# Turning each query and key tile once: high and low parts side by side, and copies that write both halves of the partitions

## The chip, the cores and the metric

The kernel runs on one core of a Trainium2 chip. The core has TensorE (PE, matrix products; PEld is its weight load), VectorE (DVE), ScalarE (ACT), GpSimd (POOL) and SyncE (SP, which issues most DMAs). SBUF is the working memory of 128 partitions, PSUM the memory of 8 banks into which PE writes. The metric is the device time in microseconds of one execution, the median of several runs.

## The reference

A two-layer backbone block on 512 latent tokens and 256 context tokens, model width 1024, head width 64. Layer 0 has two groups of heads, windowed with a sink (A) and dense (B), each with grouped queries (four query heads for one key and value head); layer 1 is differential attention with eight heads of two sub-heads. Queries and keys are normalised by their root mean square and rotated before the scores:

```
# layer 0, per group of four query heads (A; B is dense and has no sink)
qa = _rms(qa.reshape(b, n, HEADS_A, d), qn_a);  ka = _rms(ka.reshape(b, n, KV_A, d), kn_a)
qa, ka = _rope(qa, cos, sin), _rope(ka, cos, sin)
s = einsum('bqhgd,bkhd->bhgqk', q, k) * scale;  o = softmax(s) @ v
# layer 1, two sub-heads a = 0, 1 per head
s = einsum('bqhad,bkhad->bhaqk', q, k) * scale
p = softmax(s);  o = (p[:, :, 0] - lam * p[:, :, 1]) @ v
```

Each layer ends in a SwiGLU feed-forward network; all inputs and outputs are fp32.

## The kernel before, in words

All products that need more than the reduced precision of one pass are split: an operand x is held as a high part (rounded to the type fp32r) and a low part, x minus the high part. For the scores the split is folded into the contraction. A head has only 64 dimensions, so the 128 partitions of a turned tile hold two copies or two parts of the same 64 numbers. In layer 0 the query tile qt holds [high; low] along the partitions, and the key tile kT holds for j = 0 the high part of the key twice, [high; high], and for j = 1 the low part twice, [low; low]; two products with the same qt and j = 0, 1 (line 578) add up all four combinations. In layer 1 it is the other way round: kT holds [high; low] for each sub-head, and qt holds [high; high] and [low; low] (lines 715 and 716).

The tiles are made as follows. A projection (project, line 465) writes 128 tokens x 384 columns into a PSUM bank; ACT copies it to SBUF (qkv, lines 520 and 677); DVE and POOL normalise and rotate it (qy). ACT rounds the high part into qd or kd, and DVE (queries) or POOL (keys) subtracts it to get the low part (lines 525 to 530 and 685 to 689). PE then turns 128 tokens x 128 numbers at a time by a transpose against the identity identr into PSUM (qpt and kpt, lines 535, 543, 696, 702), and ACT copies the turned tile to SBUF (lines 537, 544, 698, 703), where the scores read it as qt and kT.

The order of PE's instructions is written out by hand from layer 0's sixth attention step to the end; the other engines' orders come from a planner that takes the instructions in program order as they become ready. In layer 0 one step of attention (attend0: scores into sc, softmax, four probability tiles turned into ppt and copied to Pt, values) is interleaved with quarters of the next head group's projection; a list `due` holds the turns of queries and keys (turn_q, turn_k), and one is taken at fixed places between the quarters. In layer 1 the loop over 32 steps (8 heads x 4 tiles of queries) takes in turn the scores, half a projection, the transposes of the probabilities of the step before (ppt, line 734), half a projection, its values (av, line 744), a turn (turned, which runs the function transposes of a projected tile), half a projection, and another turn.

PSUM is shared by tags: `tr_tile` hands out the banks tr0 and tr1 in turn, and qpt, kpt and layer 1's ppt take theirs from it; in layer 0 ppt takes tr0 and tr1 by the parity of its chunk (`one=kc % 2`). A bank is given to its next tile only when all readers of the one before are done. The inputs of the scores have room for some steps: six qt tiles in layer 0, five in layer 1.

Of the kernel before, what the change touches and what calls it, by code (L numbers as in the profile page):

```python
# [12 lines left out]
F32R = mybir.dt.float32r  # L13
# [6 lines left out]
P = 128  # L20
# [7 lines left out]
HD = 64  # L28
# [23 lines left out]
def bc(ap, pos, n):  # L52

    dims = [list(d) for d in ap.ap]
    return AP(ap.tensor, ap.offset, dims[:pos] + [[0, n]] + dims[pos:])
# [8 lines left out]
def backbone(es: ExitStack, tc: tile.TileContext, x, c, ctx, c_ctx, mod_w, mod_b, norm_mix_w, norm_ffn_w,  # L64
# [3 lines left out]
    nc = tc.nc  # L68
# [24 lines left out]
    def acc_tile(name, n=512, one=None):  # L93

        if one is None:
            one = turn["acc"] = 1 - turn["acc"]
        return p_1.tile([P, 512], F32, name=name, tag=f"acc{one}")[:, :n]
# [4 lines left out]
    def tr_tile(name, shape, dt=F32, one=None):  # L102
        if one is None:
            one = turn["tr"] = 1 - turn["tr"]
        return p_1.tile(shape, dt, name=name, tag=f"tr{one}")
# [10 lines left out]
    def f32(ap):  # L116
        return ap.bitcast(F32)
# [13 lines left out]
    identr = cp.tile([P, P], F32R, name="identr")  # L131
# [248 lines left out]
    def rope_tables(pool, wq, wk):  # L380

        rp = raw_tile([P, NTX, 2, HD], "rp")
        nc.sync.dma_start(rp, rope)
        w = pool.tile([P, 2, HD], F32, name="rw", tag="rw")
        nc.sync.dma_start(w[:, 0, :], dram_rows(wq))
        nc.sync.dma_start(w[:, 1, :], dram_rows(wk))
        nc.vector.tensor_scalar(w[:, 0, :], w[:, 0, :], HD ** -0.5, None, ALU.mult)
        tb = pool.tile([P, 2, NTX, 2, HD], F32, name="rt", tag="rt")
        for j in range(2):
            nc.vector.tensor_tensor(tb[:, j, :, 0, :], rp[:, :, 0, :], bc(w[:, j, :], 1, NTX), ALU.mult)  # L390
            sw = swap_pairs(w[:, j, :])
            nc.vector.tensor_tensor(tb[:, j, :, 1, :].rearrange("p t (a b) -> p t a b", b=2),
                                    rp[:, :, 1, :].rearrange("p t (a b) -> p t a b", b=2),
                                    bc(sw, 1, NTX), ALU.mult)
        return w, tb
# [64 lines left out]
    def project(ps, t, ws, c0, c1, ks=range(KT), terms=((0, 0), (0, 1), (1, 0))):  # L460

        hs = [tile_T(j, t) for j in range(2)]
        for k in ks:
            for j, z in terms:
                nc.tensor.matmul(ps, hs[j][:, k, :], ws[k // 2][z][:, k % 2, c0:c1], start=(k, j, z) == (0, 0, 0),  # L465
                                 stop=(k, j, z) == (KT - 1, 1, 0))
# [14 lines left out]
    def weights0(b, wp, subs, new_tile=raw_tile, loads=((0, 1), (), (2,), (3,))):  # L481
# [3 lines left out]
        for u in range(4):  # L485
# [13 lines left out]
            subs[u % len(subs)].tensor_sub(lo, raw, f32(hi))  # L499
            yield hi, lo  # L500

    def tables0(j, tabs, wp):
        tabs[j] = rope_tables(wp, *((ev_qn_a[0], ev_kn_a[0]) if j == 0 else (ev_qn_b[0], ev_kn_b[0])))

    def in_proj0(b, ws, tabs, wp, st, later, begun={}):

        kT = st.tile([P, 2, TOK], F32R, name="kT", tag="kT")
        vv = st.tile([P, NT, HD], F32, name="vv", tag="vv")
        qs = {}
        yield qs, kT, vv  # L510
        for t in CTX_FIRST:
            ps = begun[t] if t in begun else acc_tile("inps", 384, one=int(b == 0 and t == CTX_FIRST[-1]))
            for k in range(0, KT, 2):
                if k:
                    yield
                if b == 0 and t in CTX_FIRST[:2]:
                    continue
                project(ps, t, ws, 0, 384, range(k, k + 2))
            raw = wp.tile([P, 384], F32, name="qkv", tag="qkv", bufs=2)
            nc.scalar.copy(raw, ps)  # L520
            nc.gpsimd.tensor_copy(vv[:, t, :], raw[:, 320:384])
            y, r = rotate(raw[:, 0:320], 4, 1, t, *tabs[b // 2], wp)
            nc.gpsimd.tensor_tensor(y, y, bc(r, 2, HD), ALU.mult)
            qd = wp.tile([P, 4, 2, HD], F32R, name="qd", tag="qd", bufs=2)
            nc.scalar.copy(qd[:, :, 0, :], y[:, 0:4])
            nc.vector.tensor_sub(qd[:, :, 1, :], y[:, 0:4], f32(qd[:, :, 0, :]))
            kd = wp.tile([P, 2, 2, HD], F32R, name="kd", tag="kd", bufs=2)
            kb = bc(y[:, 4, :], 1, 2)
            nc.scalar.copy(kd[:, 0], kb)
            nc.gpsimd.tensor_sub(kd[:, 1], kb, f32(kd[:, 0]))  # L530

            def turn_q(t=t, qd=qd):
                pt = tr_tile("qpt", [P, 4, P], F32R)
                for h in range(4):
                    nc.tensor.transpose(pt[:, h, :], qd[:, h].rearrange("p a d -> p (a d)"), identr)
                qt = st.tile([P, 4, P], F32R, name="qt", tag="qt", bufs=6)
                nc.scalar.copy(qt, f32(pt))
                qs[t] = qt

            def turn_k(t=t, kd=kd):  # L540
                pk = tr_tile("kpt", [P, 2, P], F32R)
                for j in range(2):
                    nc.tensor.transpose(pk[:, j, :], kd[:, j].rearrange("p a d -> p (a d)"), identr)
                nc.scalar.copy(kT[:, :, t * P:(t + 1) * P], f32(pk))
            later += [turn_q, turn_k]
            yield

# [109 lines left out]
    class Proj1:  # L657
# [14 lines left out]
        def finish(self, t, ps):  # L672

            n, wp, kT, qs = self.width(t), self.wp.pool, self.kT, self.qs
            m, h0 = (n - P) // HD, 0 if t < NTX else 2
            raw = wp.tile([P, 384], F32, name="qkv", tag="qkv", bufs=4)
            nc.scalar.copy(raw[:, :n], ps[:, :n])  # L677
            nc.gpsimd.tensor_copy(self.vv[:, t, :], raw[:, n - P:n])
            y, r = rotate_all(raw[:, :n - P], h0, m, t, self.wc, self.tb, wp)
            nc.gpsimd.tensor_tensor(y, y, bc(r, 2, HD), ALU.mult)  # L680
            nq = m - 2
            if nq:
                qd = wp.tile([P, 2, 2, 2, HD], F32R, name="qd", tag="qd", bufs=3)
                yb = bc(y[:, 0:2], 2, 2)
                nc.scalar.copy(qd[:, 0], yb)
                nc.vector.tensor_sub(qd[:, 1], yb, f32(qd[:, 0]))
            kd = wp.tile([P, 2, 2, HD], F32R, name="kd", tag="kd", bufs=3)
            nc.scalar.copy(kd[:, :, 0, :], y[:, nq:nq + 2])
            nc.gpsimd.tensor_sub(kd[:, :, 1, :], y[:, nq:nq + 2], f32(kd[:, :, 0, :]))

            def transposes():
                if nq:
                    pt = tr_tile("qpt", [P, 2, 2, P], F32R)
                    for j in range(2):
                        for a in range(2):
                            nc.tensor.transpose(pt[:, j, a, :], qd[:, j, a].rearrange("p a d -> p (a d)"), identr)
                    qt = self.qp.tile([P, 2, 2, P], F32R, name="qt", tag="qt", bufs=5)
                    nc.scalar.copy(qt, f32(pt))
                    qs[t] = qt
                pk = tr_tile("kpt", [P, 2, P], F32R)  # L700
                for a in range(2):
                    nc.tensor.transpose(pk[:, a, :], kd[:, a].rearrange("p a d -> p (a d)"), identr)
                nc.scalar.copy(kT[:, :, t * P:(t + 1) * P], f32(pk))
            return transposes
# [452 lines left out]
    wp = Pool("mw0", "right")  # L1157
# [5 lines left out]
    for t in CTX_FIRST:  # L1163
# [4 lines left out]
        for g in range(2):  # L1168
            pt = tr_tile("npt", [P, 4, P])
# [46 lines left out]
    mods = [(0, part, n) for part in (2, 3, 4) for n in range(4)]  # L1216
    tabs = {}
    tables0(0, tabs, wp.pool)

    start.close()  # L1220
# [6 lines left out]
    even = Pool("even0")  # L1227
    due, made = [], 0
    proj = in_proj0(0, ws, tabs, wp.pool, even.pool, due, begun)
    state = next(proj)  # L1230

# [58 lines left out]
    if True:  # L1290
        for i, (b, t) in enumerate(steps):
            j = i % NT
# [3 lines left out]
            if j == 0 and b < 3:  # L1296
                ws += units
                proj = in_proj0(b + 1, ws, tabs, wp.pool, (even if b % 2 else odd).pool, due)
                nxt = next(proj)
# [30 lines left out]
            if t == 0:  # L1330
# [13 lines left out]
                wp = Pool("w0", "right")  # L1344
# [219 lines left out]
    wp = Pool("mw1", "right")  # L1564
# [44 lines left out]
    if True:  # L1609
# [117 lines left out]
        wp = Pool("w1", "right")  # L1727
# [203 lines left out]
```

## Time and profile before

| what | before |
|---|---|
| median of 3 runs | 1697.77 us (1697.59 to 1698.07) |
| span of the profiled execution, first to last instruction | 1695.6 us |
| what lies around the span, against the median | 2.2 us |
| PE busy | 1631.5 us (96%) |
| DVE busy | 1146.7 us (68%) |
| ACT busy | 937.0 us (55%) |
| POOL busy | 696.4 us (41%) |
| layer 0's attention with its projections | about 60 to 345 us |
| layer 0's feed-forward part and the way out of it | about 345 to 975 us |
| layer 1's attention with its projections | about 975 to 1300 us |

The profile is of one execution; the runs were timed without it, so the profiled execution's own time is taken as its span, and the 2.2 us beside it as constant. Busy time of PE is modelled from pipelined products: a product's duration is its latency, and the distance from one start to the next is what it costs in a full stream.

### The profile page before, as it was taken

To read this page: it belongs to the slowest core of one execution; us is meant where nothing else is said; L and a number is where in the kernel's file an instruction comes from. 1 tells how busy PE (TensorE), PEld (TensorE's weight loads), DVE (VectorE), ACT (ScalarE), POOL (GpSimd) and SP (SyncE) were. 2 spreads that over 40 slices of the span, in tenths; PEclk is the share of its full clock that TensorE was granted. 3 is DMA by queue.
4 is the path that set the end of the run, shared out by engine and by line. 5 is a ranking of instruction groups with operands and counts; after the bars stand their busy time and mean duration, and the time that the engine had idled before them with its cause. 6 is when DMAs were issued, how large, how long until landed. Compare 5 with 4: busy or idle time off the path is not lost. (4 is left out here: it accounts for less than half of the span.)

```text
span 1695.6 us, 28585 instructions
## 1 busy us (share of the span) xinstructions
PE 1631.5 (96%) x10390; PEld 1468.6 (87%) x10390; DVE 1146.7 (68%) x2014; ACT 937.0 (55%) x2011; POOL 696.4 (41%) x867
## 2 busy tenths in 40 slices
PE   6999999899999999999999989999999999999998
PEld 3977787677999999998777889999988899999887
DVE  3765656754799887767767656666666598887434
ACT  5565555745456665545554456666666555555320
POOL 2665554321346554412413366666664242221000
PEclk8999999999999999999999999999999999999999
DMA  9222221411455555439966311111112433331431
GB/s 319 69 71 74 70 70 50 164 60 38 129 167 172 164 159 162 134 108 347 296 184 189 99 43 38 48 42 44 50 45 97 125 93 102 111 101 57 137 99 62
DMA packets 218108, 194.64 MB, mean 115 GB/s; under 512 B 20016, under 2 KB 202864, under 8 KB 217968
## 3 DMA queue, kind: packets, MB, share of 16 engines
q1 hardware_dynamic: 217616, 192.62, 36.8%
q8 instruction: 81, 1.33, 0.3%
q14 instruction: 59, 0.48, 0.1%
q10 hardware_dynamic: 352, 0.21, 0.0%
HBM read 179.92 MB, written 12.87 MB: 114 GB/s over the span
## 5 line engine op out<-in xcount | busy, mean ns | idle before, releaser
L901 ACT CAST wbh<-wr 128x512 fp32r<-128x512 f32 x170 | 104.9, 621 | 130.2 <-PE p L933 73.4
L933 PE MATMUL p<-hT,wbh 128*128 128x256 f32 (+1 forms) x752 | 154.5, 299 | 0.0
L465 PE MATMUL inps<-wih,hT 128*128 128x384 f32 x512 | 144.2, 344 | 7.3 <-ACT qkv L677 7.3
L911 POOL TENSOR_TENSOR wbl<-wr,wbh 128x512 fp32r<-128x512 f32 x43 | 60.0, 1396 | 173.6 <-ACT wbh L901 173.6
L933 PEld LDWEIGHTS p<-hT,wbh 128*128 128x128 f32 x752 | 121.9, 191 | 0.2
L911 DVE TENSOR_TENSOR wbl<-wr,wbh 128x512 fp32r<-128x512 f32 x127 | 107.7, 858 | 21.0 <-ACT wbh L901 16.8
L933 PE MATMUL p<-hT,wbl 128*128 128x256 f32 (+1 forms) x376 | 111.9, 298 | 0.0
L933 PE MATMUL p<-t,wbh 128*128 128x384 f32 (+1 forms) x480 | 111.3, 318 | 0.0
L604 POOL TENSOR_SCALAR Pt<-Pt,rc 128x256 f32<-128x256 f32 (+3 forms) x96 | 74.6, 788 | 89.3 <-DVE rc L601 83.1
L231 POOL TENSOR_TENSOR modp<-modp 128x512 f32<-128x512 f32 x40 | 57.4, 1436 | 114.3 <-ACT modp L230 114.3
L465 PEld LDWEIGHTS inps<-wih,hT 128*128 128x128 f32 x512 | 93.3, 188 | 10.6 <-ACT qkv L677 9.7
L933 PE MATMUL p<-hTt,wbh 128*128 128x256 f32 (+1 forms) x480 | 101.0, 302 | 0.0
L887 POOL TENSOR_TENSOR wr<-wr 128x512 f32<-128x512 f32 x40 | 61.6, 1540 | 89.8 <-DVE ws L892 85.8
L933 PE MATMUL p<-b,wbh 128*128 128x384 f32 x368 | 93.8, 336 | 0.2 <-DVE c L961 0.2
L901 ACT CAST wbh<-ws 128x512 fp32r<-128x512 f32 x120 | 69.4, 579 | 43.1 <-PE p L933 29.0
L224 DVE SCALAR_TENSOR_TENSOR ma<-modw,cols,ma 128x256 f32<-128x256 f32 x140 | 89.2, 637 | 2.3
L592 ACT ACTIVATE Pt<-sc,nm 128x256 f32<-128x256 f32 (+3 forms) x96 | 67.6, 707 | 35.3 <-DVE nm L588 16.9
L465 PE MATMUL inps<-wil,hT 128*128 128x384 f32 x256 | 86.0, 336 | 0.0
L933 PEld LDWEIGHTS p<-t,wbh 128*128 128x128 f32 x480 | 82.9, 189 | 0.0
L911 DVE TENSOR_TENSOR wbl<-ws,wbh 128x512 fp32r<-128x512 f32 x120 | 81.7, 681 | 1.7 <-ACT wbh L901 1.6
L933 PEld LDWEIGHTS p<-hTt,wbh 128*128 128x128 f32 x480 | 78.3, 191 | 3.1 <-ACT modp L230 1.6
L230 ACT ACTIVATE modp<-modw,cols 128x256 f32<-128x256 f32 x160 | 68.4, 500 | 18.0 <-POOL ma L236 10.1
(355 smaller groups left out, 5217.9 us busy)
## 6 DMA issues: line engine op xcount, KB each, us to landing
modw<-in_mod_w_dram SPq DMA_DIRECT2D x96, 512.0 KB, 5.2
wr<-in_ffn_w_in_dram SPq DMA_DIRECT2D x176, 256.0 KB, 2.9
wdr<-in_ffn_w_out_dram SPq DMA_DIRECT2D x66, 512.0 KB, 3.7
wir<-in_od_w_in_dram SPq DMA_DIRECT2D x96, 128.0 KB, 2.3
hidm<-hid SPq DMA_DIRECT2D x44, 192.0 KB, 1.9
hr<-hidm SPq DMA_DIRECT2D x22, 192.0 KB, 3.5
x<-in_x_dram SPq DMA_DIRECT2D x8, 512.0 KB, 3.5
wir<-in_ev_w_in_dram SPq DMA_DIRECT2D x16, 256.0 KB, 3.5
```

The source lines that it names most:

```text
L224: nc.vector.scalar_tensor_tensor(acc, w[:, k], scale[k], acc, ALU.mult, ALU.add)
L230: nc.scalar.activation(pr[:, k], w[:, k], AF.Copy, scale=scale[k])
L231: nc.gpsimd.tensor_add(pr[:, 0:2], pr[:, 0:2], pr[:, 2:4])
L465: nc.tensor.matmul(ps, hs[j][:, k, :], ws[k // 2][z][:, k % 2, c0:c1], start=(k, j, z) == (0, 0, 0), stop=(k, j, z) == (KT - 1, 1, 0))
L592: turn["exp"] = nc.scalar.activation(p[:, :n], s, AF.Exp, bias=nm[:, c1], accum_out=sm[:, c1])
L604: nc.gpsimd.tensor_scalar(p[:, :n], p[:, :n], rc[:, hh:hh + 1], 1.0, ALU.mult, ALU.mult)
L887: nc.gpsimd.tensor_sub(w, raw[f, "G1"], w)
L901: nc.scalar.copy(hi, w)
L911: (nc.gpsimd if name == "G2" else nc.vector).tensor_sub(lo, raw[need[n]], f32(hi))
L933: nc.tensor.matmul(ps, w[:, k, :], H[b][h][:, k, :], start=first and k == 0 and q == 0, stop=final and k == 3 and q == 2, skip_group_check ...
```

## The change

Layer 0's keys and layer 1's queries are no longer doubled before the turn. kd (layer 0) and qd (layer 1) hold the high and the low part side by side, as the other two tiles did before, so that one transpose of 128 numbers turns both parts: [high; low] along the partitions. The doubling is done by the copy out of PSUM. A new function both_halves copies part j (64 partitions of the turned tile) twice: ACT writes it to the half of the partitions in which it lies, DVE to the other half. What the scores read is laid out as before, and PE's order is otherwise the same.

```diff
+    def both_halves(to, pt):
+        for j in range(2):
+            part = f32(pt[HD * j:HD * (j + 1)])
+            nc.scalar.copy(to[HD * j:HD * (j + 1), j], part)
+            nc.vector.tensor_copy(to[HD * (1 - j):HD * (2 - j), j], part)
...
-            kd = wp.tile([P, 2, 2, HD], F32R, name="kd", tag="kd", bufs=2)
-            kb = bc(y[:, 4, :], 1, 2)
-            nc.scalar.copy(kd[:, 0], kb)
-            nc.gpsimd.tensor_sub(kd[:, 1], kb, f32(kd[:, 0]))
+            kd = wp.tile([P, 2, HD], F32R, name="kd", tag="kd", bufs=2)
+            nc.scalar.copy(kd[:, 0], y[:, 4])
+            nc.gpsimd.tensor_sub(kd[:, 1], y[:, 4], f32(kd[:, 0]))
...
             def turn_k(t=t, kd=kd):
-                pk = tr_tile("kpt", [P, 2, P], F32R)
-                for j in range(2):
-                    nc.tensor.transpose(pk[:, j, :], kd[:, j].rearrange("p a d -> p (a d)"), identr)
-                nc.scalar.copy(kT[:, :, t * P:(t + 1) * P], f32(pk))
+                pk = tr_tile("kpt", [P, P], F32R)
+                nc.tensor.transpose(pk, kd.rearrange("p a d -> p (a d)"), identr)
+                both_halves(kT[:, :, t * P:(t + 1) * P], pk)
...
-                qd = wp.tile([P, 2, 2, 2, HD], F32R, name="qd", tag="qd", bufs=3)
-                yb = bc(y[:, 0:2], 2, 2)
-                nc.scalar.copy(qd[:, 0], yb)
-                nc.vector.tensor_sub(qd[:, 1], yb, f32(qd[:, 0]))
+                qd = wp.tile([P, 2, 2, HD], F32R, name="qd", tag="qd", bufs=3)
+                nc.scalar.copy(qd[:, :, 0, :], y[:, 0:2])
+                nc.vector.tensor_sub(qd[:, :, 1, :], y[:, 0:2], f32(qd[:, :, 0, :]))
...
-                    pt = tr_tile("qpt", [P, 2, 2, P], F32R)
-                    for j in range(2):
-                        for a in range(2):
-                            nc.tensor.transpose(pt[:, j, a, :], qd[:, j, a].rearrange("p a d -> p (a d)"), identr)
+                    pt = tr_tile("qpt", [P, 2, P], F32R)
+                    for a in range(2):
+                        nc.tensor.transpose(pt[:, a, :], qd[:, a].rearrange("p a d -> p (a d)"), identr)
                     qt = self.qp.tile([P, 2, 2, P], F32R, name="qt", tag="qt", bufs=5)
-                    nc.scalar.copy(qt, f32(pt))
+                    both_halves(qt, pt)
```

## The prediction, before the change was run

> **What bounds the kernel now.** I read the page's busy times first, then busy time by stage, then the transposes' and copies' rows, and last the order of time around single turns, because an average over the span hides which stage the change is in. In all fences times are us and mean durations ns.
>
> ```profile
> span 1695.6 us, 28585 instructions
> ...
> PE 1631.5 (96%) x10390; PEld 1468.6 (87%) x10390; DVE 1146.7 (68%) x2014; ACT 937.0 (55%) x2011; POOL 696.4 (41%) x867
> ```
>
> ```profile
> core 0: us, PE busy (x) PEld busy (x) DVE busy (x) ACT busy (x) POOL busy (x), PEclk, DMA share, GB/s
> ...
> 117.00:300.00 183.00, 172.02 (x1301) 139.01 (x1304) 110.95 (x270) 107.38 (x285) 95.86 (x149) 0.99 0.20 62
> ...
> 1002.00:1262.00 260.00, 252.51 (x1767) 242.96 (x1768) 166.90 (x340) 168.72 (x437) 173.31 (x276) 1.00 0.15 42
> ```
>
> TensorE (PE) is busy for 96% of the span. The two stages that the change touches are layer 0's attention (117 to 300 us here, after a start at 68 us) with PE at 94%, and layer 1's attention (1002 to 1262) with PE at 97%. PE's order is written by hand in both, so an instruction that is taken off PE there gives its time back, unless PE has to wait somewhere else for longer. DVE is at 61% and 64% and ACT at 59% and 65%: neither is the bound, but both are in-order queues, and an operation that becomes ready meets a busy engine more often than not.
>
> Who makes PE wait today, in 60 to 300 us (two lines) and in 975 to 1272 us (one line; columns: total us, times, longest):
>
> ```profile
> PE ppt L612 <- ACT qt L537: 4.1, 4, 2.9
> ...
> PE ppt L612 <- ACT kT L544: 1.1, 2, 0.7
> ```
>
> ```profile
> PE inps L465 <- ACT qkv L677: 7.7, 10, 1.4
> ```
>
> In layer 0 PE already waits for the copies out of qpt and kpt. The reason is the PSUM bank: the turned tiles and the transposed probabilities (ppt) share the banks tr0 and tr1, and a bank is free only when its last reader is done. In layer 1 PE waits for the copy of qkv, which the change doesn't touch.
>
> **The change part by part: what goes.** Two of four transposes go from each query turn of layer 1, and one of two from each key turn of layer 0. There are 128 and 48 transposes now, so 64 and 24 go.
>
> ```profile
> L696 PE MATMUL qpt<-identr,qd x128: 222/251/367, 987.8 to 1270.2; 128*128 128x128 f32 x128
> ```
>
> ```profile
> L543 PE MATMUL kpt<-identr,kd x48: 220/228/281, 68.4 to 299.3; 128*128 128x128 f32 x48
> ...
> L544 ACT CAST kT<-kpt x24: 361/372/393, 71.1 to 299.9; 128x256 fp32r<-128x256 f32 x24
> ```
>
> The 251 ns of one is latency, not its price: they are pipelined. The price is the distance from start to start, read off a stretch of layer 1 in which nothing waits:
>
> ```profile
> 1037.68 0.42 PEld L696 LDWEIGHTS qpt<-identr,qd 128*128 128x128 f32 x4
> 1037.71 0.54 PE L696 MATMUL qpt<-identr,qd 128*128 128x128 f32 x4
> 1038.05 0.23 PEld L702 LDWEIGHTS kpt<-identr,kd 128*128 128x128 f32 x2
> ...
> 1038.22 0.19 PEld L465 LDWEIGHTS inps<-wih,hT 128*128 128x128 f32 x1
> ...
> 1039.01 0.57 ACT L698 CAST qt<-qpt 128x512 fp32r<-128x512 f32 x1
> ...
> 1040.41 0.29 PE L702 MATMUL kpt<-identr,kd 128*128 128x128 f32 x2
> ```
>
> Four loads take 1038.05 - 1037.68 = 0.37 us and two take 0.17: 0.09 each. So layer 1 gives 64 x 0.09 = 5.8 us and layer 0 gives 24 x 0.085 = 2.0 us: 7.8 us, 0.46% of the span, and no more, since nothing else is taken off PE.
>
> **What is added.** Each turned tile was copied out by one ACT instruction. Now ACT and DVE each copy both parts (64 partitions each), the one to the same half, the other to the other half.
>
> ```profile
> L615 DVE COPY Pt<-ppt 128x512 f32<-128x512 f32 x48 | 33.0, 687 | 14.7 <-PE ppt L612 14.2
> ...
> L698 ACT CAST qt<-qpt 128x512 fp32r<-128x512 f32 x32 | 18.7, 586 | 2.7 <-PE qpt L696 2.6
> L686 DVE TENSOR_TENSOR qd<-qy,qd 128x256 fp32r<-128x256 f32 x32 | 18.7, 585 | 11.3 <-ACT qd L685 11.3
> ...
> L703 ACT CAST kT<-kpt 128x256 fp32r<-128x256 f32 x48 | 18.2, 378 | 1.2 <-PE kpt L702 1.2
> ...
> L688 ACT CAST kd<-qy 128x128 fp32r<-128x128 f32 x48 | 14.3, 299 | 15.0 <-POOL qy L680 14.8
> ...
> L737 DVE COPY PT<-ppt 128x256 f32<-128x256 f32 x32 | 13.4, 418 | 6.7 <-PE ppt L734 6.6
> L685 ACT CAST qd<-qy 128x256 fp32r<-128x256 f32 x32 | 13.0, 406 | 23.4 <-POOL qy L680 23.4
> ```
>
> No row has 64 partitions; I price a copy by its columns alone, and bound it by half of that below and by the next wider row above. ACT out of PSUM: 586 for 512 columns, 378 for 256, so 274 for 128. DVE: 687, 418, so 283. A query turn costs ACT 2 x 378 - 586 = +170 and saves 406 - 299 = 107 in the split, so +63 ns x 32 = 2.0 us; a key turn costs 2 x 274 - 372 = +176, less some 50 in its split: x 24 = 3.0 us. DVE gets 2 x 418 = 836 a query turn, less between 0.14 and 0.29 us for half of the 585 ns subtraction, about 20 us in all, and 24 x 2 x 283 = 13.6 us in layer 0. POOL's key subtraction halves, which nothing waits for often. DVE goes to about 68% and 71%: still not the bound. I take 1.0 us for PE waits behind DVE's fuller queue (between 0 and 3: late probabilities, ppt after L727, have slack of a whole step).
>
> **What is late next.** A bank is now held until the last of four copies ends. In layer 0 a key turn is followed by eight products or one quarter of the projection, then by the ppt that needs its bank, tr0:
>
> ```profile
> 128.91 0.34 PE L543 MATMUL kpt<-identr,kd 128*128 128x128 f32 x2
> ...
> 129.29 0.37 ACT L544 CAST kT<-kpt 128x256 fp32r<-128x256 f32 x1 [0.53 <-PE kpt L543]
> ...
> 130.20 0.66 PE L612 MATMUL ppt<-cst,Pt 128*128 128x128 f32 x4
> ```
>
> ```profile
> 294.64 0.37 ACT L544 CAST kT<-kpt 128x256 fp32r<-128x256 f32 x1 [1.19 <-PE kpt L543]
> ...
> 295.06 0.76 PE L612 MATMUL ppt<-cst,Pt 128*128 128x128 f32 x5 [0.46 <-ACT kT L544]
> ```
>
> At 129 the cover is 130.20 - 129.25 = 0.95 us, and the copy was done after 0.41. At 294 there is none left, and PE waited. From 117 to 300 there are 17 key turns; in nine of them, of which these are the second and the last, that ppt follows 0.5 to 1.8 us after, in the other eight after 2 us or more. The copy's own chain is at least 0.04 + two ACT copies overlapped (0.46) + a gap + one DVE copy (0.28), so 0.85 us, and DVE's current operation is waited for on top, about 0.3 us at 61% busy with operations of some 0.5 us. That is 0.2 to 0.9 us late in nine places, 0.45 in the mean: 4.0 us. The seven turns before 117 us add about 0.8.
>
> In layer 1 the cover is 1040.41 - 1038.25 = 2.16 us here at its shortest, seen about twice a head, and the new hold some 1.7 us: hidden. It is not hidden at the end, where two query turns follow at once:
>
> ```profile
> 1269.43 1.22 DVE L727 SCALAR_TENSOR_TENSOR e<-e,rt 128x768 f32<-128x768 f32 x1
> ...
> 1269.79 0.56 PEld L696 LDWEIGHTS qpt<-identr,qd 128*128 128x128 f32 x4 [0.90 <-ACT qt L698]
> 1269.79 0.75 PE L696 MATMUL qpt<-identr,qd 128*128 128x128 f32 x4 [0.76 <-ACT qt L698]
> ```
>
> DVE is in a 1.22 us operation there until 1270.65, so its two copies end at about 1271.4: 1.6 us later than today; with 0.3 us each at the turns of 988 and 1263 us, 2.2 us.
>
> **The sum.** -7.8 + 4.0 + 0.8 + 2.2 + 1.0 = +0.2 us. Of the 7.0 us of new bank waits I expect a quarter to replace waits that come anyway (PE lost 11 of 183 us in layer 0 already): -1.5. So about -1 us: the span goes from 1695.6 to about 1694.5. The median of the runs before is 1697.8, 2.2 above the span; I predict **1697**, no change to be told (0.2%, 3.4 us, is about what can be told).
>
> **Rivals.** *Everything hidden, faster.* ACT and DVE read the bank together and meet idle engines: the hold is 0.55 us plus little, the nine places cost 1 us, the end 0.8, DVE's queue 1.0: -7.8 + 2.8 = -5, so 1693. For it: the idle before both ACT copies above shows ACT waiting ready for kpt. Against it: DVE's 61%.
>
> *One chain of four, slower.* The four copies of a tile read one bank, and if no two readers of a bank are let in at once, they go ACT, DVE, ACT, DVE. A key's hold is then 4 x 0.28 + 3 gaps of 0.04 + 0.04 = 1.3 us with both engines idle, and 2.0 with two or three short waits: 1.1 us late in nine places (10), 1.8 before 117 us, and in layer 1 4 x 0.4 + 0.15 + waits of 0.8 = 2.6 against the cover of 2.16: 0.4 in some ten places (4) and 3 at the end, plus 1 for DVE. Less a quarter: -7.8 + 15 = +7, so 1705. It decides once the key's hold passes 1.4 us. For it: nothing in the trace has two engines read one bank without one depending on the other, so neither is shown. Against it: ACT and DVE could be taken at other moments.
>
> [...]
>
> **How the numbers follow.** My sum 0.37 (own range 1694 to 1701), hidden 0.32 (1691 to 1695), chain of four 0.31 (1700 to 1709). Faster by more than 0.2%, below 1694.4: 0.25 of the hidden case and 0.07 of mine. Slower, above 1701.2: 0.27 of the chain and 0.07 of mine. The rest, 0.34, is no change. The range 1692 to 1707 leaves out a tenth on each side.
>
> **What the next profile would show.** Right: 64 qpt and 24 kpt transposes, 5.8 us fewer PE slots in layer 1; waits of PE ppt L612 for kT grown from 1.1 us to about 5, with DVE as releaser; the copies of the second part on ACT starting before DVE's first ends. The hidden case: those waits stay below 2 us. The chain: ACT's second copy starts only after DVE's first, and PE qpt and kpt wait in layer 1's middle. What would make all three wrong is a reordered ACT or DVE queue that moves qkv or the exponentials by more than these copies cost.

## The result, and the profile after

The changed kernel takes 1727.7 us (1725.2 to 1728.8, 4 runs) against 1697.7 us for the kernel before: 1.0182 times as long, interval 1.0164 to 1.0199. The predicted range, 1692 to 1707, doesn't hold it. The profiled execution has a span of 1725.8 us, 30.2 more than before.

The same two views as before, now of the changed kernel: the page's busy times, and busy time by stage.

```profile
span 1725.8 us, 28576 instructions
...
PE 1631.6 (95%) x10302; PEld 1462.5 (85%) x10302; DVE 1173.0 (68%) x2126; ACT 946.4 (55%) x2067; POOL 692.7 (40%) x867
```

```profile
core 0: us, PE busy (x) PEld busy (x) DVE busy (x) ACT busy (x) POOL busy (x), PEclk, DMA share, GB/s
117.00:300.00 183.00, 161.21 (x1156) 130.32 (x1156) 107.59 (x283) 100.35 (x273) 88.52 (x141) 0.96 0.18 56
...
1002.00:1262.00 260.00, 239.14 (x1653) 228.73 (x1654) 174.24 (x381) 166.15 (x452) 165.98 (x271) 0.99 0.14 41
```

The 88 transposes are gone (10390 to 10302 products), and PE is as busy as before in total. But in the same 183 us of layer 0 it gets 1156 products done where it did 1301, and its granted clock falls from 0.99 to 0.96; in 260 us of layer 1, 1653 where it did 1767. Of these 145 and 114 products fewer, 20 and 46 are transposes of the changed tiles; the rest is work that comes later. By the starts of fixed products (the first scores and the first of the output projection, `ops`), layer 0 up to its first `ops` is 18.7 us later, and layer 1 from its first key turn to its first `ops` takes 11.3 us more. Everything between and after is unmoved, within 1 us.

The waits of PE, over 60 to 300 us (first two lines) and 975 to 1310 us, with the columns total us, times, longest:

```profile
PE ppt L616 <- DVE kT L506: 11.2, 6, 3.0
...
PE ppt L616 <- ACT qt L542: 1.6, 2, 1.4
```

```profile
PE ppt L736 <- DVE qt L506: 14.0, 7, 3.3
PE inps L465 <- ACT qkv L681: 10.9, 16, 2.5
PE qpt L698 <- DVE qt L506: 2.7, 2, 2.3
```

Both of the largest waits are new, and both are for DVE's last copy out of the bank that ppt needs. The copies themselves cost what the prediction made them by their columns (366 and 422 ns for 256 columns, 260 and 288 for 128). What stands around them is seen in the rows of DVE's copies, line 506: who kept DVE idle ahead of them, and who waited for them.

```profile
L506 DVE CAST qt<-qpt x64: 417/422/428, 1011.4 to 1302.7; 64x256 fp32r<-64x256 f32 x64
L506 DVE CAST kT<-kpt x48: 283/288/294, 70.7 to 319.3; 64x128 fp32r<-64x128 f32 x48
its engine sat idle before it (us, times) until:
  ACT qt L505: 43.1, 41
  ACT kT L505: 18.8, 17
who waited for it (us, times):
  PE ppt L616: 14.1, 7
  PE ppt L736: 14.0, 7
  ACT qt L505: 3.5, 6
  PE qpt L698: 2.7, 2
  ACT kT L505: 2.5, 5
```

DVE waits for ACT's copy 58 times, 62 us in all, and ACT for DVE's 11 times, 6 us: four copies in one chain, ACT, DVE, ACT, DVE. The program holds those waits: in the records of the instructions each copy of a turned tile after the first carries a wait for the semaphore that the one before it on the other engine raises. All 11 waits of ACT are of its second copy, of partitions 64 to 127, for DVE's first, of partitions 0 to 63 (the one at 258.19 starts 0.03 us after DVE's end): the two read no partition of the bank in common, so this program was ordered more coarsely than by the partitions read.

One key turn of layer 0 in order of time, of ACT, then of DVE (start, duration, work):

```profile
269.32 0.24 ACT L505 CAST kT<-kpt 64x128 fp32r<-64x128 f32 x1
269.63 0.48 ACT L526 COPY qkv<-inps 128x384 f32<-128x384 f32 x1
270.13 0.26 ACT L505 CAST kT<-kpt 64x128 fp32r<-64x128 f32 x1
```

```profile
269.65 0.28 DVE L506 CAST kT<-kpt 64x128 fp32r<-64x128 f32 x1
270.14 0.75 DVE L456 TENSOR_TENSOR qy<-qkv,rt 128x256 f32<-128x256 f32 x1 [0.21 <-ACT qkv L526]
270.81 1.17 DVE L454 TENSOR_TENSOR qz<-qkv,rt 128x256 f32<-128x256 f32 x2
271.91 0.27 DVE L456 TENSOR_TENSOR qy<-qkv,rt 128x64 f32<-128x64 f32 x1
272.20 0.29 DVE L506 CAST kT<-kpt 64x128 fp32r<-64x128 f32 x1
...
```

```profile
272.64 1.06 PE L616 MATMUL ppt<-cst,Pt 128*128 128x128 f32 x8 [3.05 <-DVE kT L506]
```

The four copies need 1.07 us. They take 3.2, since at each handover another operation is ahead in the next engine's queue: ACT's copy of qkv, then the whole rotation on DVE, 2.1 us. Measured from the end of the last transpose to the end of the last copy, a key's bank is held 2.99 us in the mean (0.95 before; 19 of 24 above 2 us) and a query's of layer 1 2.70 us (0.79 before; 11 of 32 above 2 us). In layer 1 most turns are held 1.95 us, and PE waits for none of these. Once a head the same queue forms, with DVE's last copy behind a 0.95 us maximum over the scores: there the hold is 4.7 us, and PE stands 1.77 us at 1088.39 and at the same place of five other heads.

The clock is the second part. After five of the stalls in layer 0 the granted clock is 0.5 for about 3.4 us; before had one such stretch there (at 198 us). Four of these stalls are for the bank; the one that ends at 163.5 us is for POOL's probabilities (Pt). Two microseconds of each of the five, with the columns of the view by stage (the 0.50 is the granted clock):

```profile
144.50:146.50 2.00, 2.00 (x12) 1.13 (x10) 0.00 (x0) 0.33 (x2) 1.56 (x2) 0.50 0.04 8
165.00:167.00 2.00, 2.00 (x10) 1.90 (x9) 1.29 (x4) 0.94 (x5) 0.73 (x2) 0.50 0.02 4
212.50:214.50 2.00, 2.00 (x12) 1.11 (x10) 0.20 (x1) 0.22 (x1) 1.84 (x3) 0.52 0.00 0
274.50:276.50 2.00, 2.00 (x8) 1.80 (x7) 1.53 (x2) 1.06 (x3) 1.15 (x3) 0.50 0.00 0
312.00:314.00 2.00, 2.00 (x11) 1.48 (x12) 0.48 (x1) 0.58 (x1) 0.88 (x1) 0.50 0.00 0
```

Summed over slices of 1 us, layer 0 loses 8.5 us of full clock, against 1.7 before. That closes its account: PE's idle time between the first scores and the first `ops` grew from 18.4 to 33.0 us (+14.6), the clock takes 6.8, the transposes there give 2 to 3 back, and the stretch is 18.2 longer. Layer 1 closes in the same way: 14.7 us more of idle time, 1.7 of the clock, and 5.1 less of PE's own work make 11.3.

### The profile page after: what moved, and what is told of

It reads as the page before. It is cut to its first block, busy times and chain, and to the rows that moved or that the text cites. A ratio compares the mean times of both kernels' runs of the same rounds, so it can differ in the third digit from the quotient of the medians.

```text
span 1725.8 us, 28576 instructions
## 1 busy us (share of the span) xinstructions
PE 1631.6 (95%) x10302; PEld 1462.5 (85%) x10302; DVE 1173.0 (68%) x2126; ACT 946.4 (55%) x2067; POOL 692.7 (40%) x867
## 3 DMA queue, kind: packets, MB, share of 16 engines
q8 instruction: 81, 1.33, 0.3%
## 5 line engine op out<-in xcount | busy, mean ns | idle before, releaser
L616 PE MATMUL ppt<-cst,Pt 128*128 128x128 f32 x400 | 58.6, 280 | 23.5 <-DVE kT L506 14.1
```

The source lines that it names most:

```text
L616: nc.tensor.transpose(pt[:, h, :], Pt[h][:, cs], ident)
```

## The experiments

Two theories went in. The *chain theory*: the four copies wait for each other over one bank, and the bank is held till the last. The *load theory*: it is the added copying, on DVE above all, that delays what PE waits for, whoever holds the bank. The ratio is to the kernel before on the same chip (medians 1694.0 to 1694.6 us), with its interval; the stages are those named above, each from one trace, so a difference of 2 or 3 us there says little. The trace before is of an execution of 1697.6 us, some 3 us above those medians, so the last two columns can add up to less than the ratio says.

| run | us | ratio | layer 0 | layer 1 |
|---|---|---|---|---|
| the change | 1727.7 | 1.0182 [1.0164, 1.0199] | +18.7 | +11.3 |
| e1_layer1_only | 1704.3 | 1.0059 [1.0044, 1.0074] | -1.5 | +9.7 |
| e2_layer0_only | 1717.1 | 1.0135 [1.0119, 1.0151] | +21.0 | +0.8 |
| e3_through_sbuf | 1703.0 | 1.0049 [1.0034, 1.0064] | +0.7 | +0.9 |
| e4_one_handover | 1722.1 | 1.0171 [1.0150, 1.0192] | +15.1 | +10.5 |
| e5_swap | 1708.2 | 1.0080 [1.0067, 1.0092] | +12.8 | +0.3 |
| e6_one_copy | 1690.8 | 0.9978 [0.9969, 0.9987] | -5.0 | -3.9 |
| e7_all_act | 1710.2 | 1.0094 [1.0080, 1.0108] | +11.1 | +0.3 |
| e8_copies_alone | 1727.0 | 1.0191 [1.0170, 1.0212] | +22.2 | +9.7 |
| e9_dve_behind | 1707.2 | 1.0074 [1.0062, 1.0086] | +7.1 | +1.8 |
| e10_dve_apart | 1703.1 | 1.0049 [1.0035, 1.0064] | +1.1 | -0.5 |
| e11_dma_swap | 1709.5 | 1.0091 [1.0078, 1.0105] | +10.6 | +2.0 |
| e12_pool_swap | 1716.9 | 1.0127 [1.0108, 1.0146] | +0.8 | +19.8 |
| e13_two_banks | 1768.8 | 1.0444 [1.0427, 1.0460] | +12.4 | +56.3 |
| e14_layer1_all_act | 1695.5 | 1.0006 [0.9997, 1.0015] | +0.6 | -1.7 |
| e15_dve_spread | 1707.1 | 1.0070 [1.0055, 1.0085] | +2.8 | +6.7 |

**One layer at a time.** e1 has the keys of layer 0 as before the change, e2 the queries of layer 1.

> Only layer 1's queries are changed; layer 0's keys are as before. Chain theory (a turned tile's four copies go ACT, DVE, ACT, DVE, each waiting for the one before, and the bank is held till the last): layer 1's share of the 30 us, read from the two traces, is 11 to 12 us, so about 1709. Load theory (the added DVE time in an in-order queue delays what PE waits for, whoever holds the bank): layer 1 gets 22 of the 36 us of added DVE time, so about 18 of the 30 us, 1716.

> Only layer 0's keys are changed; layer 1's queries are as before. Chain theory: layer 0's share of the loss in the traces is 19 us, so about 1716. Load theory: 14 of the 36 us of added DVE time, about 12 us, 1710.

The losses are 0.59% and 1.35%, together 1.94%; the change has 1.82%. The two halves add up, and each stage's loss stays with its own half. The split is the chain theory's and not the load theory's, but the chain theory had it from the change's own traces, so this places the loss and doesn't show its cause.

**The bank out of the chain.** e3 empties the bank by one ACT copy to SBUF, and makes the four copies from there:

```diff
+        mid = pool.tile(list(pt.shape), F32R, name="mid", tag="mid", bufs=3)
+        nc.scalar.copy(mid, f32(pt))
         for j in range(2):
-            part = f32(pt[HD * j:HD * (j + 1)])
+            part = f32(mid[HD * j:HD * (j + 1)])
...
```

> One ACT copy takes the turned tile out of PSUM into a tile in SBUF, and the same four copies as in the change (ACT, DVE, ACT, DVE) go from there. Chain theory: the bank is free after one copy, sooner than before the change, so the transposes' 7.8 us come back, less some for the fuller queues: 1690 to 1696. In the trace the four copies no longer wait for one another, if it was the common bank that ordered them; if they still alternate, the destination ordered them. Load theory: the load is higher than in the change by one ACT copy a turn, so 1728 to 1735.

More copying than the change, and three quarters of the loss gone: 1.33% of the time, some 22 us, was the sharing of the bank, with the half-clock stretches that came of it (3.4 us lost in layer 0 here, 8.5 in the change). Two of its waits, 60 to 300 us:

```profile
PE ppt L618 <- POOL Pt L610: 3.3, 7, 0.8
...
PE ppt L618 <- ACT mid L504: 1.3, 2, 1.0
```

The bank is held 0.83 us (keys) and 0.57 us (queries), less than before the change. The second copies of each engine, all but two of 112, no longer carry a wait for the other engine, so the common source in SBUF did not order them, and the bank had. The load theory's 1728 to 1735 is out; the chain theory's 1690 to 1696 is missed by 7 us, so something else costs too.

**One handover in place of three.** e4 orders the copies ACT, ACT, DVE, DVE.

```diff
-            nc.scalar.copy(to[HD * j:HD * (j + 1), j], part)
-            nc.vector.tensor_copy(to[HD * (1 - j):HD * (2 - j), j], part)
+            nc.scalar.copy(to[HD * j:HD * (j + 1), j], parts[j])
+        for j in range(2):
+            nc.vector.tensor_copy(to[HD * (1 - j):HD * (2 - j), j], parts[j])
...
```

> The same four copies, in the order ACT, ACT, DVE, DVE. Chain theory: one handover between the queues in place of three; the bank is held some 1.0 us (keys) and 1.6 us (queries) plus one wait for DVE, so most of the loss goes: 1700 to 1708. Load theory: the same load, 1728.

A miss for the chain theory as stated. The hold falls only to 2.18 us (keys, from 2.99) and 2.21 us (queries, from 2.70): the one handover that is left still meets a full queue. In layer 1 (975 to 1310 us) the wait moves to other tiles:

```profile
PE av L747 <- DVE PT L740: 7.2, 6, 1.3
PE ppt L737 <- DVE qt L507: 3.5, 7, 2.2
```

DVE's two copies are now together ahead of its copy of the probabilities, and the values wait for that. Two handovers fewer gained nothing that can be told (1.0171 against 1.0182).

**No handover.** e5 lets ACT copy the whole tile [high; low] and makes the other order from SBUF on DVE; e7 gives all four copies to ACT.

```diff
+        nc.scalar.copy(to[:, 0], f32(pt))
         for j in range(2):
...
+            nc.vector.tensor_copy(to[HD * (1 - j):HD * (2 - j), 1], f32(to[HD * j:HD * (j + 1), 0]))
```

> Another layout: one ACT copy takes the whole turned tile [high; low] out of PSUM, and two DVE copies write [low; high] beside it, from SBUF; the two products of the scores then add up the same four combinations. Chain theory: the bank is held by one ACT copy alone, so the transposes' 7.8 us come back: 1690 to 1693, faster than both kernels. Load theory: DVE has as many added copies as in the change, so 1715 to 1728.

> All four copies on ACT, none on DVE. Chain theory: no handover; the bank is held for four overlapped ACT copies, 0.8 us (keys) and 1.2 us (queries), near the 0.95 us that layer 0's keys have: 1695 to 1702. Load theory: DVE has less to do than before the change and ACT some 25 us more in 440 us: 1700 to 1710, with waits for qkv grown in layer 1.

Layer 1 is back to its time in both, with 0.60 and 1.77 us of hold. Layer 0 isn't: +12.8 and +11.1. Of that the clock has 6.8 us in e5 (8.5 lost against 1.7) and 3.4 in e7. In e7 the bank is part of it: four copies on one engine still hold a key's bank for 1.86 us, and PE's ppt waits 7.8 us for them over 75 to 340 us, where it waited 1.1 before. In e5 the hold is short (0.79 us), and the waits that grew are for the exponentials (PE's sc for ACT's Pt, 6.8 us where it was 2.7) and for the normalised probabilities (ppt for POOL's Pt, 6.3 where it was 3.5). The prediction had named moved exponentials as what would make all three of its cases wrong; why they moved in e5 is open. e5 confirms neither theory by its total, and e7's total is at the upper edge of the load theory's range, but with the loss in the other layer.

**The transposes alone, and the copies alone.** e6 removes the transposes and copies the tile by one ACT instruction of the old size, which reads it twice (`nc.scalar.copy(to, bc(f32(pt), 1, 2))`); it leaves out the products of a high with a low part. e8 keeps the transposes of before, and puts the change's four copies behind them.

> The transposes are removed as in the change, but one ACT copy of the old size takes the tile out, by reading it twice: both places get [high; low], and the cross products of high and low are left out. It shows what the removed transposes alone are worth with the copies as they were. Both theories: 7.8 us by the start-to-start distance, 1690. If PE's time there were hidden by other waits: 1697.

> The transposes are as before the change (doubled parts), and the change's four copies, ACT, DVE, ACT, DVE, take the tiles out. It shows the copies' cost without the transposes' gain. Both theories: the change's 30 us plus the 7.8 us that it saves, about 1735. If the transposes' gain is lost in the longer waits for the bank: 1728.

The transposes, with the halved splits that go with them, are worth 0.22% [0.13, 0.31], 3 to 4 us here, where the prediction's start-to-start distances gave 7.8. In the change they are worth nothing that can be told: 1.0191 with them, 1.0182 without.

**What DVE's work costs without the bank.** e9 is the kernel before with two DVE copies from the finished tile into scratch that nobody reads; in e10 they read a constant, in e15 the tiles kd and qd from before the turn.

```diff
...
                 nc.scalar.copy(kT[:, :, t * P:(t + 1) * P], f32(pk))
+                idle = wp.tile([P, 2, P], F32R, name="idle", tag="idle", bufs=1)
+                for j in range(2):
+                    nc.vector.tensor_copy(idle[HD * (1 - j):HD * (2 - j), j], f32(kT[HD * j:HD * (j + 1), j, t * P:(t + 1) * P]))
...
```

> The kernel before (its transposes and its single ACT copy), and behind each turned key of layer 0 and query of layer 1 two DVE copies of 64 partitions from the finished kT or qt into a scratch tile that nobody reads. It puts on DVE what the swap variant put there, behind ACT's copy, without anyone who waits for it and without a longer hold of the bank. Chain theory: no bank is held longer, so 1694 to 1698, at most 0.2% over before. Load theory: DVE's 64 more pairs (about 37 us of busy time), each at the head of DVE's queue until ACT's copy is done, delay PE as in the swap variant: 1704 to 1710, with most of the loss in layer 0's attention. If this one is at no loss while the swap variant lost 13 us, the loss there came from the scores that read the swapped halves late.

> As the kernel with two DVE copies behind ACT's, but the DVE copies read the constant identity instead of kT or qt, so they wait for nobody: the load on DVE alone. Chain theory: 1694 to 1697. Load theory in its form of work (DVE's busy time counts): as the run with the copies behind ACT's, 1704 to 1710. Load theory in its form of blocked queue heads (the wait for ACT counts): 1694 to 1697 here and 1704 to 1710 there.

> The kernel before with two DVE copies of 64 partitions beside each key turn of layer 0 and query turn of layer 1, as in the run behind ACT's copy, but they read kd and qd, which are done before the turn: the same DVE work in the same stages, at no queue head that waits for ACT's copy of the turn. If the wait at the queue's head is what the run behind ACT's copy lost 7 us by in layer 0's attention: layer 0 within 2 us of before and the total 1694 to 1699. If it is the work: layer 0 plus 5 to 9 us and the total 1703 to 1708.

e10 is no test of these stages: the planner drew its copies to where they were ready, out of both, as their rows (first and last start) show:

```profile
L704 DVE CAST idle<-identr x64: 286/289/1823, 941.4 to 989.8; 64x256 fp32r<-64x256 f32 x64
L547 DVE CAST idle<-identr x48: 219/222/234, 4.9 to 19.5; 64x128 fp32r<-64x128 f32 x48
```

It is slower all the same, by 0.49%: its trace loses 6.8 us between the two stages, where the 64 copies lie. So work on DVE can cost time there too.

e15's copies do lie in the stages, and they wait for almost nothing:

```profile
L704 DVE CAST idle<-qd x64: 286/290/1849, 979.5 to 1278.7; 64x256 fp32r<-64x256 f32 x64
L547 DVE CAST idle<-kd x48: 220/223/1859, 66.1 to 292.9; 64x128 fp32r<-64x128 f32 x48
its engine sat idle before it (us, times) until:
  POOL kd L530: 0.4, 1
```

It loses as much in all as e9, whose copies kept DVE idle for ACT:

```profile
L704 DVE CAST idle<-qt x64: 286/289/1986, 997.6 to 1281.6; 64x256 fp32r<-64x256 f32 x64
L547 DVE CAST idle<-kT x48: 220/222/752, 73.5 to 307.7; 64x128 fp32r<-64x128 f32 x48
its engine sat idle before it (us, times) until:
  ACT qt L701: 29.2, 16
  ACT kT L544: 12.9, 9
```

So some 29 us of DVE work (64 x 0.29 + 48 x 0.22) cost some 12 us of the time in both runs, with or without the waits for ACT. In e15's layer 1 (975 to 1310 us) PE waits 11.2 us for qkv where it waited 7.7; that DVE is later with the rotation, and ACT with the copy that follows in its queue, is the likely path and is not shown.

```profile
PE inps L465 <- ACT qkv L680: 11.2, 10, 2.3
```

The two stages share the loss differently: layer 0 has 7.1 us in e9 and 2.8 in e15, which lies between the two answers that e15 was to decide between. The clock accounts for 3.4 of these 4.3 us, with 5.1 us lost in e9's layer 0 and 1.7 in e15's. So the totals speak for the work, and layer 0 alone decides nothing.

**The swap on other engines.** As e5, with the two copies from SBUF as transfers on SP's queue (e11) or on POOL (e12).

> The change's single transposes, one ACT copy of the whole turned tile [high; low], and the other order [low; high] by two transfers from SBUF to SBUF on SP's queue: no more work on ACT or DVE than before, the bank held for one ACT copy. If the loss of the swap variant lay in DVE's queue, both stages keep the transposes' gain except where a scores product follows its turn within the transfer's time of some 2 us or more: 1690 to 1696. If it lay in the swapped halves coming late, this is slower, since a transfer takes longer than a DVE copy: layer 1, where the least distance from turn to scores is 2.2 us, loses 1 us or more in some of 32 steps, 1700 to 1730.

> As the swap variant (one ACT copy of the whole turned tile, then the other order from SBUF), with POOL in place of DVE for the two copies. If DVE's queue was what lost 13 us in layer 0: layer 0 within 3 us of before, and the total 1692 to 1699. If it was the swapped halves coming late, POOL's slower copies make it the same or worse: 1706 to 1720. POOL is busy 173 of 260 us in layer 1, so there some 30 us more may come to its limit: plus 0 to 5 us.

POOL shows that layer 0 doesn't suffer from swapped halves that come later (+0.8, with the last copy ending 1.54 us after ACT's in the mean, where e5 had 1.05), and that layer 1 has no room on POOL: 64 copies of 396 ns there make PE wait for the weights' low parts (10.4 us) and for kd (9.9 us).

```profile
PE inps L465 <- ACT qkv L680: 10.6, 16, 1.9
PE inps L465 <- POOL wil L371: 10.4, 6, 1.7
PE kpt L703 <- POOL kd L691: 9.9, 7, 2.3
```

e11 puts no copy on ACT, DVE or POOL beyond ACT's one, and loses 10.6 us in layer 0. One wait of 3.2 us for a transfer (1.9 us from issue to landing, in the median) is in its trace, and a half-clock stretch behind it; half-clock stretches cost layer 0 5.1 us more than before in all. The rest lies in waits for POOL and ACT in another order than before, and is not explained.

**Two banks.** e13 turns the tile into both banks, ACT reads one and DVE the other, so no copy waits for the other engine.

```diff
...
+                    pt2 = tr_tile("qpt", [P, 2, P], F32R, one=1 - turn["tr"])
+                    for p in (pt, pt2):
+                        for a in range(2):
+                            nc.tensor.transpose(p[:, a, :], qd[:, a].rearrange("p a d -> p (a d)"), identr)
...
```

> The turned tile is made twice, in the two banks of the turns: ACT makes its two copies from the one, DVE its two from the other, so neither waits for the other, and as many transposes are issued as in the kernel before. All four copies still read PSUM, and DVE's load is the change's. Chain theory: the loss is the waits of the two engines for each other across one bank, so the hold falls from 2.7 to 3.0 us to about 1 us and the time is near that of before with a DVE load beside it: 1697 to 1708. Load theory, or a slowness of the copies out of PSUM themselves: as the change's copies with the transposes of before, 1723 to 1730.

Its time lies outside both ranges and says nothing on the theories: with both banks taken, the key turn right behind each query turn waits, 42 us in all over 975 to 1400 us.

```profile
PE kpt L707 <- DVE qt L505: 42.1, 31, 3.2
```

But the hold falls as the chain theory said, from 2.99 to 1.26 us (keys) and from 2.70 to 1.37 us (queries). In one turn the same four copies, side by side, take some 0.9 us:

```profile
1160.24 0.73 ACT L504 CAST qt<-qpt 64x256 fp32r<-64x256 f32 x2
```

```profile
1160.27 0.86 DVE L505 CAST qt<-qpt 64x256 fp32r<-64x256 f32 x2 [2.35 <-PE qpt L701]
```

**A version to keep?** e14 has layer 0 as before and, in layer 1, all four copies on ACT.

> Layer 0's keys as in the kernel before; layer 1's queries turned once with all four copies on ACT, which cost layer 1 nothing in the run that had this in both layers. Chain theory: no handover, and layer 1 keeps some of its 40 transposes less: 1692 to 1696, at best 2 us below before; a loss of more than 0.2% would say that ACT's extra 1.1 us per query are on PE's path. Load theory (added work on the copying engine delays PE): 1698 to 1702.

The same as before, within 0.15%. No version that computes the whole reference beat the kernel before; e6's 3 to 4 us are what fewer transposes can win here, and each way of doubling behind the turn used them up.

## Why the prediction was wrong

**What held.** The durations by columns; the transposes that go; the place (PE's ppt waiting for a turned tile's last copy, in both layers); that waits in layer 0 come with DVE as releaser. The sign that the prediction set for its third rival, *one chain of four*, is what the trace shows: ACT's second copy starts only after DVE's first. Its other sign, PE's qpt and kpt waiting in layer 1's middle, is not seen: there it is ppt that waits.

**The steps that failed,** in order of size:

- *What is late next.* The sum had the copies overlap in pairs and waited 0.3 us for DVE, 0.45 us late in nine places. They overlap nowhere; the hold is 2.99 us for keys. The places were right: PE's ppt stalls at seven of the nine key turns, where at most six products of a projection (1.1 us) lie between, and at none of the eight with 2 us or more of cover, which is the work that PE has before it needs the bank. What failed is how late the last copy is: 2.0 us in the mean of the seven, 14.1 in all, where the sum had 4.0. Layer 1 was said to be hidden behind 2.16 us at a hold of 1.7. At the usual hold of 1.95 it is, but not once a head: there eight score products and twelve of a projection, some 3 us, lie between, the hold is 4.7, and the waits come to 14.0 us, for which the sum had nothing. The terms 4.0 + 0.8 + 2.2 = 7 measured some 20 us (the change with before's transposes against e9, 1.0191 - 1.0074, and the change against e3, 1.0182 - 1.0049), the half-clock stretches included.
- *The rival had the mechanism and the wrong size.* Its 1.3 to 2.0 us for a key gave each handover a short wait; the rows show whole operations, up to 2.1 us of rotation. A copy that was handed between two engines' queues waited for what each had in front, and the mean busy share (61%) said too little: the rotation comes just when the turn does.
- *DVE's queue.* 1.0 us, with a bound of 3; e9 and e15 measured about 12 us for less DVE work than the change's. "Not the bound" was read as "nearly free".
- *The transposes.* 7.8 us against 3 to 4 in e6. In e6's layer 1 PE's time without idle time and lost clock is 268.4 us where it was 274.0, so 5.6 us came off there, as the sum had it (5.8), and its idle time is the same (12.1 us); one more half-clock stretch took 1.7 back. In layer 0 the same figure is 237.8 where it was 237.3: the 2.0 us aren't seen. Why not, and where the rest went, is open.
- *Not in the sum at all:* the half-clock stretches behind stalls, 6.8 us in layer 0; they are also part of the 20 us above.

The measured parts add up, as percentages: 1.2 to 1.3 for the bank, 0.7 for DVE's work, less 0.2 for the transposes, is 1.7 to 1.8, against 1.82. The bank's share is itself a difference of these runs, so the one test in this is the sum without the bank: DVE's work less the transposes is 0.5, and e3 measured 0.49. It does not give e5 (0.8 measured) or e11 (0.9 measured, -0.2 by the sum); their layer 0 stays open. Each edit makes the planner order ACT, DVE and POOL anew, which may be the cause there, but no run shows it.

## What to carry to other kernels

Before you split one copy out of PSUM over two engines, look whether the program makes two readers of one bank wait for each other: here each handover then cost not the copy but whatever stood in the other engine's queue (copies of 1.07 us took 3.2), and the bank was held through all of it. Let one engine empty the bank in one instruction, and do the rest from SBUF; here that took away three quarters of the loss (1.82% to 0.49%), though the kernel before was still faster. And price work added to an engine at 60% busy by what follows it in that engine's queue in the same stage, not at zero: here some 29 us of it on DVE cost some 12.

## What the runs showed of the hardware

In the traces of the two kernels the granted clock is 0.5 or 1.0, and within each trace its changes lie whole multiples of 3.41 us apart. In the changed kernel's layer 0 the stretches at 0.5 begin at 144.33, 164.81, 212.60, 274.04 and 311.58 us. Each lasts 3.41 us, so 1.7 us are lost on top of the stall ahead of it, and their distances (20.48, 47.79, 61.44 and 37.54) are 6, 14, 18 and 11 times 3.41 us. Cut into slots of 3.41 us from one of these changes, the trace has by its records PE idle for 2.1, 2.0, 2.3, 2.0 and 2.8 us in the five slots just ahead of them, and for about 1.5 us or less in every other slot of this stage. The stall of 2.2 us at 227.2 lies across two slots, with 1.25 and 0.92 us in them, and no half clock follows. Nor does it follow the six of 1.77 us in layer 1, each of which lies in one slot. In both traces, from 50 us on, all ten slots at full clock with 1.97 us or more of idle time were followed by half clock; of the others one was (846.4 us in the kernel before, 1.67 us idle), and up to 1.84 us (1291.2 in the changed kernel) passed without it. What sets the clock is not shown.

DVE's copy of 64 partitions took 222 ns (128 columns) and 289 ns (256) out of SBUF (medians of e9 and e10), and 288 and 422 out of PSUM (the change).
